# One decoder block on one core: the bias rows on GpSimd's queue head by head, and rstd spread by transposes of its repeated column

## The chip, the core and the metric

The kernel runs on one core of a Trainium2 chip. The core has five engines that run side by side, each through its own instruction stream in order: TensorE (PE, with its weight loads listed as PEld), VectorE (DVE), ScalarE (ACT), GpSimd (POOL) and SyncE (SP). They meet through semaphores. Sixteen DMA engines move data between DRAM and the core's memory; transfers are handed to them by the streams of SP and POOL. The metric is the device time of one execution in microseconds; less is better.

## What is computed

One layer of a decoder trunk on 512 tokens of width 1024, all in float32. Cut to what matters here:

```python
h = rmsnorm(x, g_pre_mix)
ca, cb, q, k, v, pu, gl = split_cols(h @ w_in)
y_conv = conv_module(ca, cb, ...)          # GLU, causal depthwise conv of 31 taps, LayerNorm, swish, 512 -> 1024
o = diff_attention(q, k, v, rel_bias, lam_p, subln_g)
    # 4 heads, two softmax maps each; logits = q k^T / 8 + rel_bias[bucket(i - j)], causal
    # attn = softmax_0 - lambda * softmax_1;  o = rmsnorm(attn @ v, subln_g) * (1 - lambda_init)
y_pool = pool_mixer(pu, ...)               # causal window means of 2, 4, 8, 16 tokens, minus the token
merged = sigmoid(gates) * (y_conv, o @ w_attn_out, y_pool), summed
x = x + rmsnorm(merged @ w_out, g_post_mix)
x = x + rmsnorm(relu(rmsnorm(x) @ w_mlp_in)**2 @ w_mlp_out, g_post_mlp)
x = x + sigmoid(x @ w_ple_gate) * (p @ w_ple_proj)
```

The bias of a head depends on the distance i - j alone, so one row of 512 numbers per head holds it. Each rmsnorm and the LayerNorm needs one number per token, rstd = (mean of squares + eps) ** -0.5.

## The kernel before

Activations lie with features on the 128 partitions and the 512 tokens along the free axis, so a 512 x 1024 activation is eight tiles of 128 x 512. Every matrix is cut into chunks of 128 x 1024 numbers (512 KB), 144 of them, which come in order through the class `Weights`: `load` (L71) issues a chunk's DMA on SP's queue into a tile called `raw`, and `split` (L87) makes two float32r tiles of it, `wh` by a copy on ACT (L90) and `wl`, the rest, by a subtraction on DVE (L94). There are three `raw` tiles (`N_RAW`) and three pairs `wh`/`wl` (`N_SPLIT`) in turn, so the load of chunk n waits until chunk n - 3 has been split, and the split of chunk n until TensorE is through with chunk n - 3. A product is three matmuls (`mm3`, L153 to L156): high by high, low by high, high by low.

The order of the projections is a string, `ORDER` (L16): q and k of the first head, the first two convolution chunks (side by side), V, pooling, and so on. The V projection (`project_v`, L660) uses four chunks, V0 to V3, each for all four blocks of tokens, 24 matmuls a chunk. Between the matmuls a planner (`tick`, L246) drops steps of other work into the program: attention first, the convolution's taps (L570) second. After the hand-ordered start (up to `start.close()`, L382) a list scheduler with its own estimate of times sets the order of each engine's stream; nothing is reordered on the chip.

**The bias** (L371 to L380, L427 to L433). The rows of the four heads are made by one matmul with a one-hot matrix (L374) and copied by ACT into `rel_r`, 4 x 640 numbers (L375). `rel_r` takes one of the three `raw` tiles, so a weight chunk waits until it has been read. A DMA on SP's queue writes it to DRAM as `rel_d` (L377); a second one, behind it, repeats each row 128 times into `rep_d` (L380), 4 x 128 x 640 numbers or 1.31 MB, in one instruction whose outermost dimension is the four heads. `load_bias(h)` (L427) then reads head h's 128 x 512 bias tile with a row step of 639 numbers, which shifts each row by one against the row before; the tile has two buffers. The attention's steps add it in L454 on DVE.

**rstd** (`rstd_from` L198, `rstd_steps` L206). Four matmuls with a column of ones sum the squares (L211); DVE scales and adds eps (L201); POOL raises to -1/2 (L203); then, one per 128 tokens, a float32 matmul of rstd's column, repeated 128 times as the stationary operand, against the identity puts rstd into every partition (L216). This runs eleven times: at the start, once per head, once in the LayerNorm, twice on halves of the tokens after W_out and twice after the MLP, and once before the MLP. Seven of them are of four blocks of 128 tokens, four are of two.

Of the kernel before, what the change touches and what calls it, by code (L numbers as in the profile page):

```python
# [9 lines left out]
F32 = mybir.dt.float32  # L10
# [24 lines left out]
P = 128  # L35
S = 512
# [3 lines left out]
NH = 4  # L40
# [71 lines left out]
def block_kernel(ctx: ExitStack, tc: tile.TileContext, xT, pT, wts, pool_w, par, rel_bias, onehot, out):  # L112
    nc = tc.nc
# [4 lines left out]
    ap = ctx.enter_context(tc.tile_pool(name="ap", bufs=N_ACT))  # L118
# [3 lines left out]
    dr = ctx.enter_context(tc.tile_pool(name="dr", bufs=1, space=bass.MemoryType.DRAM))  # L122
# [11 lines left out]
    def act_tile(name, dt=F32, tag=None, pool=None, n=S):  # L134
        uid[0] += 1
        tag = tag or OWN.get(name, "a")
        return (pool or ap).tile([P, n], dt, tag=tag, name=f"{name}_{uid[0]}", bufs=BUFS.get(tag))

    def bank(tag="mm"):
        uid[0] += 1  # L140
        return ps.tile([P, S], F32, tag=tag, name=f"{tag}_{uid[0]}")
# [17 lines left out]
    start = ExitStack()  # L159
# [23 lines left out]
    ident = cp.tile([P, P], F32, name="ident")  # L183
# [14 lines left out]
    def rstd_from(ssq, inv_n, n, name):  # L198

        c = small(n, name + "c")  # L200
        nc.vector.tensor_scalar(out=c, in0=ssq, scalar1=inv_n, scalar2=EPS, op0=ALU.mult, op1=ALU.add)  # L201
        r = small(n, name + "r")
        nc.gpsimd.tensor_tensor(out=r, in0=c, in1=neghalf[:, 0:n], op=ALU.pow)  # L203
        return r

    def rstd_steps(sq, lo, n, inv_n, got, tag="at"):  # L206


        b = bank(tag)
        for j in range(n):  # L210
            nc.tensor.matmul(out=b[:, j:j + 1], lhsT=sq[:, lo + j * P:lo + (j + 1) * P], rhs=ones_col,  # L211
                             start=True, stop=True)
        r = rstd_from(b[:, 0:n], inv_n, n, "pe")
        yield
        for j in range(n):
            nc.tensor.matmul(out=b[:, j * P:(j + 1) * P], lhsT=r[:, j:j + 1].to_broadcast([P, P]),  # L216
                             rhs=ident, start=True, stop=True)
        got(b[:, 0:n * P])


# [61 lines left out]
    for kt in range(2):  # L282
        h, l = act_tile("ph", F32R), act_tile("pl", F32R)
# [41 lines left out]
    chunk[0] = 2  # L325
    x_rB = []
    steps = rstd_steps(ssum, 0, 4, 1.0 / D, x_rB.append)
    next(steps)
    project_p(6)
# [5 lines left out]
    for kt in range(KT + 1):  # L335
        if kt < KT:
            nc.vector.tensor_tensor(out=x_t[kt], in0=x_t[kt], in1=x_rB[0], op=ALU.mult)  # L337
        if kt > 0:
            h, l = act_tile("xnh", F32R, "xn", xnp), act_tile("xnl", F32R, "xn", xnp)
# [31 lines left out]
    rel_r = rawp.tile([NH, 640], F32, tag="raw", name="rel_r")  # L371
    nc.vector.memset(rel_r, NEG)
    b = bank("at")
    nc.tensor.matmul(out=b[0:NH, :], lhsT=rb_sb, rhs=oh_sb, start=True, stop=True)  # L374
    nc.scalar.copy(out=rel_r[:, 0:S], in_=b[0:NH, :])  # L375
    rel_d = dr.tile([NH, 640], F32, name="rel_d")
    nc.sync.dma_start(out=rel_d, in_=rel_r)  # L377

    rep_d = dr.tile([NH, P, 640], F32, name="rep_d")
    nc.sync.dma_start(out=rep_d, in_=bass.AP(tensor=rel_d.tensor, offset=rel_d.offset, ap=[[640, NH], [0, P], [1, 640]]))  # L380

    start.close()  # L382

# [43 lines left out]
    def load_bias(h):  # L427
        t = act_tile("bias")
        src = rep_d[h]
        nc.sync.dma_start(out=t, in_=bass.AP(tensor=src.tensor, offset=src.offset + P - 1, ap=[[639, P], [1, S]]))  # L430
        return t

    biases = [load_bias(0)]  # L433

    qk = []

    def attention():
# [68 lines left out]
        def normalize(h):  # L506
            sq, o = state["o"]

            def scaled(rB):
                nc.vector.scalar_tensor_tensor(out=o, in0=o, scalar=sub_g, in1=rB, op0=ALU.mult, op1=ALU.mult)  # L510
                hl = act_tile("oh", F32R), act_tile("ol", F32R)
                mul_split(*hl, o)
                o_hl[h] = hl
            state["fin", h] = rstd_steps(sq, 0, 4, 1.0 / P, scaled)
            next(state["fin", h])
# [5 lines left out]
        for i in range(n + 3):  # L521
            h, qb = divmod(i, 4)
            if i < n:
                while len(qk) <= h:
                    yield None
                if qb == 0 and h + 1 < NH:
                    biases.append(load_bias(h + 1))
                logits(i)
                yield 2.5 * (qb + 1) / 4 + 0.2
            if 0 < i <= n:  # L530
                combine(i - 1)
                yield 0.66 * ((i - 1) % 4 + 1) / 4 + 0.2
            if 2 < i <= n + 2 and (i - 3) % 2 == 1:
                values(i - 3)
                yield 0.3
                if (i - 3) % 4 == 3:
                    normalize((i - 3) // 4)
                    yield 0.3
            if 1 < i <= n + 1:
                transpose(i - 2)  # L540
                yield 0.66 * ((i - 2) % 4 + 1) / 4 + 0.1
            if i % 4 == NORM_LAG % 4 and i >= NORM_LAG:
                finish((i - NORM_LAG) // 4)
                yield 1.4
# [32 lines left out]
    def conv_norm():  # L577
# [16 lines left out]
        yield 2.5  # L594
        c_rB = []
        steps = rstd_steps(csq, 0, 4, 1.0 / S, c_rB.append)
        next(steps)
        for z in range(WAIT_LN):
# [160 lines left out]
    for kt in range(KT):  # L759
        t = act_tile("x")  # L760
# [7 lines left out]
    def bank2():  # L768
        turn2[0] += 1
        return bank(("mm", "at")[turn2[0] % 2])  # L770
# [96 lines left out]
    def one_tile(src):  # L867
        wh, wl = next_chunk()
        b = bank2()
        for kt in range(KT):  # L870
            mm3(b, wh[:, kt * P:(kt + 1) * P], wl[:, kt * P:(kt + 1) * P], *src[kt], kt == 0, kt == KT - 1)
        return b

    f = [act_tile("f", tag=t) for t in spare]
# [26 lines left out]
    for quarter in range(4):  # L901
# [10 lines left out]
        if quarter < 3:  # L912
            for m in range(KT):
                b = one_tile(s_hl)
# [9 lines left out]
    for m in range(KT):  # L924
        t = act_tile("proj2")
# [13 lines left out]
    for m in range(4, KT - 1):  # L939
        b = one_tile(x2)  # L940
        finish(m, b, slice(0, S))
    wh, wl = next_chunk()
    for sl in HALVES:
        b = bank2()
# [115 lines left out]
```

## Time and profile before

| what | value |
|---|---|
| time, median of 3 runs | 850.94 us (849.89 to 852.63) |
| the profiled execution | 850.82 us, span on the core 849.0 us |
| PE busy | 837.4 us, 99% of the span |
| DVE busy | 505.4 us, 60% |
| ACT busy | 349.2 us, 41% |
| POOL busy | 24.2 us, 3% |
| mean granted TensorE clock | 0.996 of full speed |
| DMA | 89.11 MB, mean 105 GB/s |

The span runs from the first to the last instruction on the core; the 1.8 us by which the execution's time is longer lie around it. Times below are microseconds from the span's start. A matmul in a dense stream is listed with a duration longer than its share, because matmuls are pipelined: what counts is the distance from one start to the next, 0.23 us for 512 columns at the full clock.

### The profile page before, as it was taken

The page shows a single profiled execution, that of the slowest core. Times are in us where ns is not written, and L with a number is a line of the kernel's source. Part 1 is how long each engine was busy: PE and PEld are TensorE (multiplying, and loading weights), DVE is VectorE, ACT ScalarE, POOL GpSimd, SP SyncE. Part 2 cuts the span into 40 slices and gives each one's busy share as a digit, 9 for nine tenths or more (in the row PEclk, how much of TensorE's full clock was granted, in tenths as well). Part 3 has the DMA queues.
Part 4 walks back from the last instruction along what each step waited for, and adds up shares of the span by engine and source line. Part 5 has one row for each costly group of instructions (what it writes and reads, how often), then busy time and mean ns, then how long its engine had stood idle before and what let it go on. Part 6 is the DMA issues. An engine that isn't in the chain of part 4 may idle for free.

```text
span 849.0 us, 10743 instructions
## 1 busy us (share of the span) xinstructions
PE 837.4 (99%) x4216; PEld 710.0 (84%) x4216; DVE 505.4 (60%) x835; ACT 349.2 (41%) x564; POOL 24.2 (3%) x57
## 2 busy tenths in 40 slices
PE   9979999999999999999999999999999999999998
PEld 7758888888888888888999888888888888889997
DVE  5839769976669995658367642343344433435772
ACT  6625426464552323653455542332134312325341
POOL 2100000010000000000000000000000000000000
PEclk9989999999999999999999999999999999999999
DMA  8353322232122223256202523222222222222311
GB/s 288 130 203 114 112 100 75 74 113 75 52 79 94 76 99 100 84 190 208 89 27 80 184 68 116 100 100 100 99 96 90 89 98 100 100 74 76 125 56 69
DMA packets 27951, 89.11 MB, mean 105 GB/s; under 512 B 3160, under 2 KB 3544, under 8 KB 27900
## 3 DMA queue, kind: packets, MB, share of 16 engines
q1 hardware_dynamic: 27260, 86.32, 30.3%
q0 software_dynamic: 640, 2.10, 0.6%
q8 instruction: 33, 0.54, 0.3%
q14 instruction: 18, 0.15, 0.1%
HBM read 84.20 MB, written 5.52 MB: 106 GB/s over the span
## 4 chain that ended last, share of the span: by engine, by line
PE 96%; DMA 2%; DVE 1%; ACT 1%; SPq 0%; issue 0%; ACTq 0%
PE mm L154 21%; PE mm L155 21%; PE mm L156 21%; PE at L154 9%; PE at L155 9%; PE at L156 9%; DMA raw<-in_wts_dram 2%; PE at L216 1%; PE at L211 1%; PE at L450 1%; PE at L448 1%; PE at L481 1%; DMA p<-in_pT_dram 0%; DMA rel_d<-rel_r 0%; DVE x L337 0%; DVE xnl L150 0%
## 5 line engine op out<-in xcount | busy, mean ns | idle before, releaser
L90 ACT CAST wh<-raw 128x1024 fp32r<-128x1024 f32 (+1 forms) x144 | 148.8, 1040 | 337.8 <-PE mm L155 153.7
L94 DVE TENSOR_TENSOR wl<-raw,wh 128x1024 fp32r<-128x1024 f32 (+1 forms) x144 | 173.6, 1210 | 112.9 <-ACT wh L90 112.5
L156 PE MATMUL mm<-xnh,wl 128*128 128x512 f32 x352 | 138.0, 392 | 0.1
L155 PE MATMUL mm<-xnl,wh 128*128 128x512 f32 x352 | 137.5, 391 | 0.0
L154 PE MATMUL mm<-xnh,wh 128*128 128x512 f32 x352 | 136.9, 392 | 0.0
L570 DVE SCALAR_TENSOR_TENSOR acc<-u,par_sb,acc 128x512 f32<-128x512 f32 x116 | 82.4, 752 | 0.1
L154 PEld LDWEIGHTS mm<-xnh,wh 128*128 128x128 f32 x352 | 66.1, 188 | 14.3 <-ACT xnh L149 0.9
L156 PEld LDWEIGHTS mm<-xnh,wl 128*128 128x128 f32 x352 | 66.1, 188 | 14.2 <-DVE wl L94 0.5
L155 PEld LDWEIGHTS mm<-xnl,wh 128*128 128x128 f32 x352 | 66.1, 188 | 13.6 <-DVE xnl L150 0.4
L154 PE MATMUL mm<-sh,wh 128*128 128x512 f32 (+1 forms) x152 | 54.5, 359 | 0.0
L155 PE MATMUL mm<-sl,wh 128*128 128x512 f32 (+1 forms) x152 | 54.5, 358 | 0.0
L156 PE MATMUL mm<-sh,wl 128*128 128x512 f32 (+1 forms) x152 | 54.2, 357 | 0.0
L154 PE MATMUL at<-sh,wh 128*128 128x512 f32 (+1 forms) x144 | 53.0, 369 | 0.0
L156 PE MATMUL at<-sh,wl 128*128 128x512 f32 (+1 forms) x144 | 52.9, 367 | 0.0
L154 PE MATMUL at<-xgh,wh 128*128 128x512 f32 (+1 forms) x144 | 52.9, 367 | 0.0
L155 PE MATMUL at<-xgl,wh 128*128 128x512 f32 (+1 forms) x144 | 52.7, 366 | 0.0
L156 PE MATMUL mm<-xgh,wl 128*128 128x512 f32 (+1 forms) x144 | 52.7, 366 | 0.0
L155 PE MATMUL at<-sl,wh 128*128 128x512 f32 (+1 forms) x144 | 52.7, 368 | 0.0
L154 PE MATMUL mm<-xgh,wh 128*128 128x512 f32 (+1 forms) x144 | 52.7, 366 | 0.0
L156 PE MATMUL at<-xgh,wl 128*128 128x512 f32 (+1 forms) x144 | 52.7, 366 | 0.0
L155 PE MATMUL mm<-xgl,wh 128*128 128x512 f32 (+1 forms) x144 | 52.6, 365 | 0.0
L154 PEld LDWEIGHTS mm<-sh,wh 128*128 128x128 f32 x152 | 28.6, 188 | 4.6
(240 smaller groups left out, 1531.0 us busy)
## 6 DMA issues: line engine op xcount, KB each, us to landing
raw<-in_wts_dram SPq DMA_DIRECT2D x140, 512.0 KB, 3.2
x<-in_xT_dram SPq DMA_DIRECT2D x16, 256.0 KB, 6.1
proj_d<-proj POOLq DMA_DIRECT2D x8, 256.0 KB, 4.0
proj<-proj_d SPq DMA_DIRECT2D x8, 256.0 KB, 4.5
out_dram<-pg SPq DMA_DIRECT2D x7, 256.0 KB, 2.0
rep_d<-rel_d SPq DMA_DIRECT2D x1, 1280.0 KB
raw<-in_wts_dram SPq DMA_DIRECT2D x4, 256.0 KB, 5.3
bias<-rep_d SPq DMA_DIRECT2D x4, 256.0 KB, 4.5
```

The source lines that it names most:

```text
L90: i = self.nc.scalar.copy(out=wh[:, sl], in_=src)
L94: i = self.nc.vector.tensor_tensor(out=wl[:, sl], in0=src, in1=wh[:, sl].bitcast(F32), op=ALU.subtract)
L154: nc.tensor.matmul(out=o, lhsT=sh, rhs=mh, start=first, stop=False)
L155: nc.tensor.matmul(out=o, lhsT=sh, rhs=ml, start=False, stop=False)
L156: nc.tensor.matmul(out=o, lhsT=sl, rhs=mh, start=False, stop=last)
L211: nc.tensor.matmul(out=b[:, j:j + 1], lhsT=sq[:, lo + j * P:lo + (j + 1) * P], rhs=ones_col, start=True, stop=True)
L216: nc.tensor.matmul(out=b[:, j * P:(j + 1) * P], lhsT=r[:, j:j + 1].to_broadcast([P, P]), rhs=ident, start=True, stop=True)
L448: nc.tensor.matmul(out=lg[m][:, 0:nn], lhsT=q[m][:, cols], rhs=k[m][:, 0:nn], start=True, stop=False)
L450: nc.tensor.matmul(out=lg[m][:, 0:nn], lhsT=ql[m][:, cols], rhs=k[m][:, 0:nn], start=False, stop=True)
L481: nc.tensor.transpose(out=tp[:, j * P:(j + 1) * P], in_=e[:, j * P:(j + 1) * P], identity=ident)
L570: nc.vector.scalar_tensor_tensor(out=t, in0=u[:, k:k + S], scalar=pcol(w0 + k), in1=t, op0=ALU.mult, op1=ALU.add)
```

## The change

Two things are changed. First, the stores of the bias rows (`rel_d`), the repeats and the loads of the bias tiles are issued by GpSimd instead of SP, and the one repeat of all heads is four, each 128 x 640 numbers (328 KB) into a DRAM tile of its own; the repeat of head h + 1 is issued in the code after the load of head h. Second, the spreading matmul of `rstd_steps` becomes `nc.tensor.transpose`, the same instruction with its transpose flag on: the repeated column is the data, the identity the other operand.

```diff
@@ rstd_steps
         for j in range(n):
-            nc.tensor.matmul(out=b[:, j * P:(j + 1) * P], lhsT=r[:, j:j + 1].to_broadcast([P, P]),
-                             rhs=ident, start=True, stop=True)
+            nc.tensor.transpose(out=b[:, j * P:(j + 1) * P], in_=r[:, j:j + 1].to_broadcast([P, P]), identity=ident)
         got(b[:, 0:n * P])
@@ block_kernel
     rel_d = dr.tile([NH, 640], F32, name="rel_d")
-    nc.sync.dma_start(out=rel_d, in_=rel_r)
-
-    rep_d = dr.tile([NH, P, 640], F32, name="rep_d")
-    nc.sync.dma_start(out=rep_d, in_=bass.AP(tensor=rel_d.tensor, offset=rel_d.offset, ap=[[640, NH], [0, P], [1, 640]]))
+    nc.gpsimd.dma_start(out=rel_d, in_=rel_r)
+
+
+    rep_d = [dr.tile([P, 640], F32, name=f"rep_d{h}") for h in range(NH)]
+
+    def repeat_rows(h):
+        nc.gpsimd.dma_start(out=rep_d[h], in_=bass.AP(tensor=rel_d.tensor, offset=rel_d.offset + 640 * h,
+                                                      ap=[[0, P], [1, 640]]))
+
+    repeat_rows(0)
@@ load_bias
         src = rep_d[h]
-        nc.sync.dma_start(out=t, in_=bass.AP(tensor=src.tensor, offset=src.offset + P - 1, ap=[[639, P], [1, S]]))
+        nc.gpsimd.dma_start(out=t, in_=bass.AP(tensor=src.tensor, offset=src.offset + P - 1, ap=[[639, P], [1, S]]))
+        if h + 1 < NH:
+            repeat_rows(h + 1)
         return t
```

The scheduler then places things anew. On SP's queue, around the loads of the weight chunks of the V projection, there stood (raw_433 is V0, raw_439, raw_500 and raw_506 are V1 to V3):

```order
L76 DMA raw_384<-in_wts_dram 128x1024
L76 DMA raw_433<-in_wts_dram 128x1024
L377 DMA rel_d<-rel_r 4x640
L380 DMA rep_d<-rel_d 512x1x640
L76 DMA raw_439<-in_wts_dram 128x1024
L76 DMA raw_500<-in_wts_dram 128x1024
L76 DMA raw_506<-in_wts_dram 128x1024
L430 DMA bias_357<-rep_d 128x512
L430 DMA bias_680<-rep_d 128x512
```

In the changed kernel the same place of SP's queue reads (V0 to V3 are now raw_437, raw_443, raw_504 and raw_510):

```order
L76 DMA raw_388<-in_wts_dram 128x1024
L76 DMA raw_437<-in_wts_dram 128x1024
L76 DMA raw_443<-in_wts_dram 128x1024
L76 DMA raw_504<-in_wts_dram 128x1024
L76 DMA raw_510<-in_wts_dram 128x1024
```

Four transfers have left the queue; raw_443 takes the tile that `rel_r` held, so its load waits for the store of `rel_d` to land. On POOL's stream of the changed kernel, where before only memsets stood behind the last store of `proj_d` (the projected p), there now stands:

```order
L348 DMA proj_d<-proj_323 128x512
L417 MEMSET ql_1195 64x512
L417 MEMSET ql_1196 64x512
L376 DMA rel_d<-rel_r 4x640
L382 DMA rep_d_354<-rel_d 128x640
L382 DMA rep_d_355<-rel_d 128x640
L382 DMA rep_d_356<-rel_d 128x640
L382 DMA rep_d_357<-rel_d 128x640
L435 DMA bias_360<-rep_d_354 128x512
L435 DMA bias_684<-rep_d_355 128x512
L629 MEMSET pu_788 128x16
```

The scheduler has put all four repeats in a row; the first waits for `rel_d` to land, the first bias load for the first repeat. On TensorE, in the V projection, the first chunk's matmuls for all four blocks of tokens stood together; these are the last of V0 and the first of V1 before:

```order
L155 MATMUL mm_525<-wl_436,xnh_274 128x512
L156 MATMUL mm_525<-wh_435,xnl_275 128x512
L154 MATMUL mm_526<-wh_435,xnh_269 128x512
L155 MATMUL mm_526<-wl_436,xnh_269 128x512
L156 MATMUL mm_526<-wh_435,xnl_270 128x512
L154 MATMUL mm_526<-wh_435,xnh_274 128x512
```

At the same place, twelve matmuls after the start of V0 (wh_439), the changed kernel already wants V1 (wh_445), and twelve later one half of V2 (wh_506), before it comes back to V0:

```order
L155 MATMUL mm_529<-wl_440,xnh_274 128x512
L156 MATMUL mm_529<-wh_439,xnl_275 128x512
L154 MATMUL mm_528<-wh_445,xnh_283 128x512
L154 MATMUL mm_529<-wh_445,xnh_283 128x512
L155 MATMUL mm_528<-wl_446,xnh_283 128x512
L156 MATMUL mm_528<-wh_445,xnl_284 128x512
```

V1 is wanted twelve matmuls earlier than before; the number of matmuls is the same. On DVE, from the split of V1 on, there stood before:

```order
L94 TENSOR_TENSOR wl_442<-raw_439,wh_441 128x1024
L570 SCALAR_TENSOR_TENSOR acc_540<-u_495,par_sb,acc_540 128x512
L570 SCALAR_TENSOR_TENSOR acc_79_542<-u_495,par_sb,acc_79_542 128x512
L570 SCALAR_TENSOR_TENSOR acc_540<-u_495,par_sb,acc_540 128x512
L94 TENSOR_TENSOR wl_503<-raw_500,wh_502 128x1024
L454 ISA lg_690,mx_688<-at_682,bias_357 128x128
```

and in the changed kernel:

```order
L94 TENSOR_TENSOR wl_446<-raw_443,wh_445 128x1024
L94 TENSOR_TENSOR wl_507<-raw_504,wh_506 128x1024
L565 SCALAR_TENSOR_TENSOR u_499<-sg_501,mm_449 128x512
L577 SCALAR_TENSOR_TENSOR acc_544<-u_499,par_sb,acc_544 128x512
L461 ISA lg_695,mx_693<-at_687,bias_360 128x128
```

The first use of the bias stands right behind V2's split and one tap of the convolution; V3's split, wl_513, stands 21 rows behind it (before, wl_509 stood 10 rows behind it).

## Rows read from the trace of the kernel before

**Rows 1.** The page: busy us by engine; ACT's copies (busy, mean ns | idle before).

```profile
PE 837.4 (99%) x4216; PEld 710.0 (84%) x4216; DVE 505.4 (60%) x835; ACT 349.2 (41%) x564; POOL 24.2 (3%) x57
...
L90 ACT CAST wh<-raw 128x1024 fp32r<-128x1024 f32 (+1 forms) x144 | 148.8, 1040 | 337.8 <-PE mm L155 153.7
```

**Rows 2.** The page: the chain that ended last, share by engine.

```profile
PE 96%; DMA 2%; DVE 1%; ACT 1%; SPq 0%; issue 0%; ACTq 0%
```

**Rows 3.** Stages: length, PE, PEld, DVE, ACT, POOL busy (count); clock, DMA share, GB/s.

```profile
51.00:57.00 6.00, 0.15 (x1) 0.15 (x1) 0.17 (x1) 1.25 (x2) 0.00 (x0) 0.82 0.43 136
57.00:62.00 5.00, 5.00 (x13) 3.92 (x14) 5.00 (x10) 3.01 (x4) 0.00 (x0) 0.54 0.55 186
62.00:103.00 41.00, 41.00 (x184) 34.03 (x183) 37.48 (x74) 19.47 (x38) 0.00 (x0) 1.00 0.37 120
103.00:200.00 97.00, 97.00 (x466) 81.27 (x465) 76.65 (x147) 48.80 (x89) 5.27 (x12) 1.00 0.26 89
```

**Rows 4.** TensorE in time: start, us, line, tiles, count [idle before, releaser].

```profile
48.06 0.39 PE L154 MATMUL mm<-wh,xnh 128*128 128x512 f32 x1
...
50.55 0.39 PE L156 MATMUL mm<-wh,xnl 128*128 128x512 f32 x1
56.85 2.08 PE L154 MATMUL mm<-wh,xnh 128*128 128x512 f32 x4 [5.91 <-ACT wh L90]
...
61.91 0.39 PE L154 MATMUL mm<-wh,xnh 128*128 128x512 f32 x1
```

**Rows 5.** The chain that ended last, in time: start, us, what.

```profile
37.09 0.59 ACT rel_r L375
37.70 1.47 DMA rel_d<-rel_r
39.18 0.72 SPq L380
40.00 15.68 DMA raw<-in_wts_dram
```

**Rows 6.** SP's queue: what it waited for: us in total, times, longest.

```profile
SPq L430 <- DMA rep_d<-rel_d: 8.3, 1, 8.3
...
SPq L430 <- DVE mx L454: 3.9, 2, 2.9
```

**Rows 7.** Stages of 1 us, columns as in rows 3.

```profile
36.00:37.00 1.00, 1.00 (x6) 0.84 (x5) 0.94 (x5) 0.94 (x2) 0.00 (x0) 1.00 1.02 410
44.00:45.00 1.00, 1.00 (x6) 0.84 (x5) 0.00 (x0) 0.00 (x0) 0.00 (x0) 1.00 0.26 102
```

**Rows 8.** Spreading matmuls and attention's transposes in the chain: start, us, count.

```profile
162.87 0.44 PE at L481 x4
...
191.96 0.89 PE at L216 x8
...
430.72 0.45 PE at L216 x4
```

**Rows 9.** Stores of proj_d on POOL: ns of one issue min/median/max, first and last start.

```profile
L349 POOL DMA_DIRECT2D proj_d<-proj x8: 542/542/731, 18.3 to 33.4; - x8
```

**Rows 10.** DMAs of proj_d, eight POOL stores and eight SP loads: issue to landing.

```profile
DMA to landing us min/median/max: 2.5/4.5/5.2
```

**Rows 11.** Weight chunks, 10 to 110 us: the same column.

```profile
DMA to landing us min/median/max: 3.1/3.9/15.7
```

**Rows 12.** The bias tiles' loads: the same column.

```profile
DMA to landing us min/median/max: 4.4/4.5/4.6
```

**Rows 13.** DVE in time, from V0's split to V4's.

```profile
38.65 2.36 DVE L94 TENSOR_TENSOR wl<-raw,wh 128x1024 fp32r<-128x1024 f32 x2 [0.20 <-ACT wh L90]
...
56.83 1.23 DVE L94 TENSOR_TENSOR wl<-raw,wh 128x1024 fp32r<-128x1024 f32 x1 [9.97 <-ACT wh L90]
...
61.09 0.29 DVE L454 CUSTOM_DVE_ANT_0 lg<-at,bias 128x128 f32<-128x128 f32 x1
...
68.25 1.23 DVE L94 TENSOR_TENSOR wl<-raw,wh 128x1024 fp32r<-128x1024 f32 x1
```

## The prediction

> **What bounds the kernel now.** I read the page's busy times first, then the chain of work that ended last, then the stretches in which TensorE was not at its pace. TensorE is busy for 99% of the span and no other engine for more than 60% [rows 1], and 96% of the chain is TensorE's [rows 2]. So time comes off only where TensorE waits, runs at a lower clock, or does fewer or shorter instructions; a queue that is relieved elsewhere pays nothing.
>
> There is one place where it waits and slows. In a table by stage TensorE does one matmul in the 6 us from 51 to 57, the clock falls, and it stands at 0.54 of full speed from 57 to 62 and at 1.00 after that [rows 3]. In order of time the last matmul of the V projection's first chunk ends at 50.94 (50.55 and 0.39), and the next starts at 56.85, after 5.91 us, released by ACT's copy of the second chunk, V1 [rows 4]. The chain in order of time says why [rows 5]: ACT finishes `rel_r` at 37.68, its store lands at 39.18, SP issues the repeat, and the load of V1, issued right behind at 40.00, takes 15.68 us to land, where the median load takes 3.9 [rows 11]. SP itself waited 8.3 us for the repeat before it could load the first bias tile [rows 6]. The DMA share in those microseconds shows the cause: 0.26 and 102 GB/s, at 44, against 1.02 and 410 GB/s at 36 [rows 7]. A quarter of sixteen engines is four: the repeat with its four heads outermost runs on four of them, 1.31 MB at 102 GB/s being 12.8 us, and V1's share on those four stands behind it in the same queue.
>
> **The change, part by part.** *The stall.* The repeat leaves SP's queue, so V1's load has nothing ahead of it. It still waits for `rel_d`, since it takes `rel_r`'s tile. POOL issues that store at 37.7 when ACT is done [rows 5]; a store issue takes POOL 0.54 us, at most 0.73 [rows 9]. How long 10 KB take from POOL's queue no row shows. The lower bound is the 1.47 us that the same bytes took from SP's queue [rows 5], the upper one the 5.2 us of the slowest of the DMAs of `proj_d`, 256 KB each [rows 10]; I take their 2.5 us minimum, because the DMA engines are nearly idle then. So `rel_d` lands at 40.2 and V1's load is issued there. Alone it takes 3.9 us [rows 11]. Now it shares the engines with the repeats; 512 KB at 410 GB/s are 1.3 us, so an equal share adds 1.3 us: V1 lands at 45.4 and its copy, 1.04 us [rows 1], ends at 46.5. The new order wants it twelve matmuls after V0's start, where the trace has 48.06 [rows 4]. V1 is in time by 1.6 us, its low part (1.23 us on DVE [rows 13]) by about 0.8. V2 follows 1.3 to 2.6 us behind V1 and is wanted twelve matmuls later, at 50.8. So I forecast no stall: 5.91 us come off.
>
> *The slow clock after it.* From 56.85 to 61.91 TensorE starts twelve matmuls in 5.06 us [rows 4]; at the 0.23 us of a dense stream (184 in 41.00 us make 0.22 [rows 3], short ones among them) they would take 2.76. Without the idle stretch ahead of it the clock has no reason to fall: 2.3 us come off. Together 8.2 us.
>
> *The bias behind it.* In DVE's new order V3's split stands behind the first uses of the bias, so a late bias now holds up TensorE where it did not before. V3's low part is wanted 64 matmuls after the 48.06, at 62.6. Before, DVE took from the first L454 at 61.09 to the end of the next split behind the softmax, 69.48, or 8.4 us [rows 13], so the bias must be there by 54.2. The repeats: four issues by POOL from 40.2, to 42.4 (0.73 each: 43.1), 1.31 MB together with the three loads of V1 to V3, 1.57 MB, at 410 GB/s 7.0 us, done by 47.4; then the bias, 4.5 us from issue to landing [rows 12], by 51.9. That is 2.3 us to spare, and costs nothing. This takes all sixteen engines for a repeat of 128 rows; POOL's stores of `proj_d`, 128 rows too, ran among others at 1.02 share [rows 7].
>
> *POOL's stream.* Behind the later bias loads (heads 2 and 3, which wait until DVE is through with an earlier head) stand memsets and POOL's power step of the next rstd. Before, SP stood at the same two waits for 3.9 us in all, 2.9 at most [rows 6]; POOL is busy for 3% [rows 1], and what stands behind is made well ahead of its use. Zero, and at most 2.9 if that lead were gone.
>
> *Does DVE stand in the way?* While POOL issued the `proj_d` stores DVE was busy most of the time (0.94 at 36 [rows 7]), and the slowest issue took 0.73 us against 0.54 [rows 9]. The Trainium skill, SBUF — State Buffer, section "SBUF: two separate sides", speaks against the change here: it warns that a DMA issued from GpSimd has its descriptors written by GpSimd's cores, which DVE locks out while it runs in a two-port mode, and gives about 620 ns for such a DMA alone and about 3100 ns under a DVE copy. An estimate from that page's two figures: six issues at 2.5 us more each bring the bias 15 us later, to 67, and the time to about 854. The trace does not bear it out, by the 0.73 us above; and DVE ends a stretch of work at 41.0, after which it sat idle 9.97 us in one piece before 56.83 [rows 13].
>
> *The spreads.* A set of four spreading matmuls is eight passes and 0.89 us on TensorE; four transposes of 128 x 128 in the attention, float32 too and against the same identity, are four passes and 0.44 us; a set of two spreads is 0.45 [rows 8]. Seven sets of four save 0.45 each and four of two 0.225: 4.05 us, all on TensorE's path. The bounds are nothing, if a repeated column is fed as slowly as before, and 4.05; I take the upper, since the transposes are the same size and type.
>
> **The sum.** 850.82 of the profiled execution less 5.91, 2.3 and 4.05 is 838.6. The execution is within 0.12 us of the median, so I take 838.6 for the new median.
>
> **The rivals.** *V1 is still late.* If `rel_d` lands only after 5.2 us, at 42.9, and V1's load takes twice its 3.9, it lands at 50.7, its copy ends at 51.8, and TensorE idles 3.7 us from 48.06; with the slow clock's 2.3 that is 6.0 back: 844.6. For it: POOL's stores did take 4.5 us in the median. Against: these were 25 times as large, on busy engines. Chance 0.13.
>
> *The spreads stay at eight passes.* The change would not do what it says there: 842.6. Chance 0.05.
>
> *The bias comes last.* `rel_d` at 42.9, the issues at 0.73, a repeat as slow as the slowest load (15.7 us) and 4.5 for the bias: 66.0. TensorE then waits for V3's split from 62.6 to 74.4, 11.8 us, with 2.3 of slow clock behind: 852.7, no change. Against: that landing was the four-engine queue itself. Chance 0.06.
>
> *Few engines for a repeat* (slower). If the descriptors that POOL makes for a source with row step zero go to few engines at 102/4 = 25.6 GB/s each, four engines give 12.8 us from 41, the bias at 58.5 and a stall of 4.3, with the clock 6.6: 845.2. Two engines take 25.6 us, the bias lands at 71, TensorE waits 17, and with the clock's 2.3 the time is 858. It passes the time before once the stall is over 9.9 us, so below three engines. For it: the old repeat used four of sixteen. Against: its outermost dimension was four, the new one's is 128. Chance 0.04 for the slower side.
>
> *The transposes let the clock fall.* If after each of eleven sets the clock fell as after the stall, 2.3 us each, 25 us come back: 864. The attention's 40 transposes lie in stages with the clock at 1.00 [rows 3], which speaks against it. The Trainium skill, TensorE: Matmul & The Clock Gate, Part 4, holds that a transpose does not count as TensorE being busy; by that rule this rival would be likelier, but the sets last 0.44 us between dense matmuls, and the trace does not agree with a fall. Chance 0.01.
>
> **How the numbers follow.** The forecast has 0.71. The range reaches up to a late V1 and to four engines, 845.5, and down to 837.0, about what the runs scatter; that holds the forecast, the late V1 and the eight passes, 0.89 in all and less what I don't see. Within 0.3% (848.4 to 853.5, about what a measurement of this kernel can tell from no change) lies the late bias, 0.06. Slower are few engines and the clock, 0.05. Faster 0.89.
>
> **What would show it.** In the profile after, TensorE's order of time without a gap between 45 and 68 and the clock at 1.00 there; V1's load landing in about 5 us; the repeats with a DMA share near 1 from 41 to 48; the first bias use on DVE near 52; L216 with half its count and 0.44 us a set. It would be wrong if TensorE waits for ACT's copy of V1 or DVE's split of V3, which the idle time of their matmuls names, or if L216 keeps its count.

## The result, and the profile after

| | before | changed |
|---|---|---|
| time, median | 851.03 us (849.89 to 852.63, 4 runs) | 840.22 us (839.25 to 841.20, 4 runs) |
| span of the profiled execution | 849.0 us | 837.8 us |
| mean granted TensorE clock | 0.996 | 0.999 |

The ratio is 0.9877, 95% interval 0.9858 to 0.9896: faster by 10.8 us where 12.2 had been forecast; the time lies in the range, 1.6 us above the forecast.

The page of the changed kernel, its span, the busy times, and the chain's shares, beside [rows 1, 2]:

```profile
span 837.8 us, 10679 instructions
...
PE 830.7 (99%) x4180; PEld 703.5 (84%) x4180; DVE 504.8 (60%) x835; ACT 348.7 (42%) x564; POOL 29.1 (3%) x66
...
PE 93%; DVE 3%; issue 1%; DMA 1%; POOL 1%; ACT 0%; SPq 0%; POOLq 0%
```

TensorE lists 36 matmuls fewer, and 3% of the chain is now DVE's, where it was 1%. The stages, columns as in [rows 3]:

```profile
46.00:51.00 5.00, 5.00 (x24) 4.14 (x23) 1.92 (x2) 1.85 (x3) 1.39 (x6) 1.00 1.02 416
51.00:57.00 6.00, 6.00 (x28) 4.99 (x27) 5.18 (x16) 2.92 (x11) 0.00 (x0) 1.00 0.40 145
57.00:62.00 5.00, 5.00 (x23) 4.13 (x22) 5.00 (x12) 3.12 (x6) 0.00 (x0) 1.00 0.09 18
62.00:95.00 33.00, 31.73 (x141) 26.04 (x140) 30.28 (x55) 15.47 (x27) 0.68 (x2) 1.00 0.37 125
```

From 51 to 57 TensorE does 28 matmuls instead of one, and from 57 to 62 it does 23 instead of 13, at the full clock: the stall and the slow stretch are gone. A new gap stands between 62 and 95, 1.27 us in one piece. The chain shows where it comes from (start, us, what):

```profile
37.64 1.83 DMA rel_d<-rel_r
...
46.54 6.00 DMA bias<-rep_d
...
52.57 0.29 DVE lg L461
...
66.85 1.99 DVE acc L577 x3
68.83 0.61 DVE vl L150
69.49 0.51 PE mm L154
```

The bias lands at 52.54, DVE works through the first attention steps, convolution taps and weight splits in its row, and reaches the low part of V's first output (`vl`) at 68.83. Until that is made, the bank (the piece of TensorE's output memory) that holds V's sums is not free, and the next projection wants it. TensorE's row at that place, as in [rows 4]:

```profile
67.82 0.40 PE L457 MATMUL at<-k,ql 128*128 128x512 f32 x1
69.49 0.51 PE L154 MATMUL mm<-xnh,wh 128*128 128x512 f32 x1 [1.27 <-DVE vl L150]
```

The spreads, with the least, median and greatest duration in ns, answer to [rows 8]: 36 where 72 were listed, weight loads of 135 ns where the median was 190; the kernel before first, the changed one below:

```profile
L216 PEld LDWEIGHTS at<-ident,per x72: 185/190/192, 18.4 to 804.4; 128*128 128x128 f32 x72
L216 PE MATMUL at<-ident,per x72: 270/275/376, 18.5 to 804.5; 128*128 128x128 f32 x72
...
L216 PEld LDWEIGHTS at<-ident,per x36: 133/135/137, 18.6 to 793.3; 128*128 128x128 f32 x36
L216 PE MATMUL at<-ident,per x36: 270/272/323, 18.6 to 793.4; 128*128 128x128 f32 x36
```

The chain lists seven sets of four (start, us), here the first two:

```profile
18.76 0.54 PE at L216 x4
...
184.77 0.44 PE at L216 x4
```

ACT's copies of V1 and V2 (start, us, idle time before) show when their loads landed, at 43.28 and 47.57:

```profile
43.28 1.05 ACT L90 CAST wh<-raw 128x1024 fp32r<-128x1024 f32 x1 [4.03 <-DMA raw<-in_wts_dram]
47.57 1.05 ACT L90 CAST wh<-raw 128x1024 fp32r<-128x1024 f32 x1 [3.24 <-DMA raw<-in_wts_dram]
```

### The profile page after: what moved, and what is told of

The parts are those of the page before. It is cut to its first block, busy times and chain, and to the rows that moved or that the text cites. A ratio compares the mean times of both kernels' runs of the same rounds, so it can differ in the third digit from the quotient of the medians.

```text
span 837.8 us, 10679 instructions
## 1 busy us (share of the span) xinstructions
PE 830.7 (99%) x4180; PEld 703.5 (84%) x4180; DVE 504.8 (60%) x835; ACT 348.7 (42%) x564; POOL 29.1 (3%) x66
## 4 chain that ended last, share of the span: by engine, by line
PE 93%; DVE 3%; issue 1%; DMA 1%; POOL 1%; ACT 0%; SPq 0%; POOLq 0%
PE mm L154 21%; PE mm L155 20%; PE mm L156 20%; PE at L154 10%; PE at L155 10%; PE at L156 9%; DVE acc L577 1%; PE at L211 1%; DMA bias<-rep_d 1%; PE at L488 1%; PE at L457 0%; PE at L455 0%; PE at L216 0%; DVE x L336 0%; DVE wl L94 0%
```

## The experiments

The theory at this point: the gain has two parts that add up, the repeat no longer on four of the DMA engines ahead of V1's load, and the spreads at half their passes; and the new wait behind the V projection takes 1.27 us of it back. The rivals: that one part gave it all; that leaving SyncE's queue, not the form of the repeat, did it; and, for the new wait, that DVE has too much work there whatever the bias does. The first four kernels below ran on one chip beside the kernel before, the last three on another chip, so between the two groups the ratios to the kernel before are what is compared.

### Each part alone

Without the transposes (the bias rows as in the changed kernel):

```diff
-            nc.tensor.transpose(out=b[:, j * P:(j + 1) * P], in_=r[:, j:j + 1].to_broadcast([P, P]), identity=ident)
+            nc.tensor.matmul(out=b[:, j * P:(j + 1) * P], lhsT=r[:, j:j + 1].to_broadcast([P, P]),
+                             rhs=ident, start=True, stop=True)
```

> The bias rows on GpSimd's queue head by head, the spread of rstd still by fp32 products. Theory (the two parts add up, each on TensorE's path): the stall in the V projection (5.9 us) and the slow clock after it (2.3 us) stay away, the new 1.27 us wait behind the V projection stays, and the spreads cost their eight passes: 840.2 + 4.05 = 844.3 us. Rival (the spreads lie beside other work and the queue gave it all): 840 to 841 us.

Measured: 843.75 us, ratio 0.9933 (0.9921 to 0.9945), 6.7 us less than the 850.48 of the kernel before on that chip. TensorE's gaps from 24 us on are one:

```profile
70.99 0.50 PE L154 MATMUL mm<-xnh,wh 128*128 128x512 f32 x1 [2.33 <-DVE vl L150]
```

The stall is gone here too, and the wait behind V is 2.33 us, where 1.27 had been expected. The profiled execution took 846.58 us, 2.8 more than the median, so this is not the wait of a usual one. DVE's row at the first use of the bias says what differs; in the changed kernel (the second line) the idle time is 0.27:

```profile
54.06 0.29 DVE L462 CUSTOM_DVE_ANT_0 lg<-at,bias 128x128 f32<-128x128 f32 x1 [1.97 <-DMA bias<-rep_d]
...
52.57 0.29 DVE L461 CUSTOM_DVE_ANT_0 lg<-at,bias 128x128 f32<-128x128 f32 x1 [0.27 <-DMA bias<-rep_d]
```

The transposes alone (the bias rows as before the change): the same diff the other way round, in the kernel before.

> Only the spread by transposes, all bias DMAs on SyncE's queue as before. Theory: the stall and the slow clock are as before, 11 sets save 4.05 us: 851.0 - 4.05 = 847.0 us, L216 36 instead of 72 matmuls. Rival (the spreads lie beside other work): 851 us. Rival (transposes let TensorE's clock fall): above 851 us, with a granted clock under 1.00 in stretches other than the one before.

Measured: 845.95 us, ratio 0.9956 (0.9944 to 0.9968), 4.5 us less. Its stages (stretch, length, TensorE busy and count, clock, DMA share, GB/s):

```profile
51.00:57.00 6.00, 0.84 (x4) 0.85 0.38 139
57.00:62.00 5.00, 4.18 (x10) 0.50 0.66 236
...
95.00:830.00 735.00, 735.00 (x3746) 1.00 0.29 97
```

Its one long gap, in TensorE's row (start, us, what, in brackets the idle time before it and what ended it):

```profile
57.82 2.07 PE L154 MATMUL mm<-wh,xnh 128*128 128x512 f32 x4 [5.98 <-ACT wh L90]
```

Stall and slow clock stand as before, and from 95 to 830, where all sets of transposes but the first lie, the clock is 1.00: it did not fall behind them. By the medians the parts give 6.7 and 4.5, together 11.3, against 10.8 of the whole change; by the ratios 5.7 and 3.7, together 9.4, against 10.5. They add up within the intervals, and that either part gave it all is ruled out.

### Queue or form

The changed kernel with every bias DMA back on SyncE's queue, the repeat still one per head:

```diff
-    nc.gpsimd.dma_start(out=rel_d, in_=rel_r)
+    nc.sync.dma_start(out=rel_d, in_=rel_r)
...
-        nc.gpsimd.dma_start(out=rep_d[h], in_=...)
+        nc.sync.dma_start(out=rep_d[h], in_=...)
...
-        nc.gpsimd.dma_start(out=t, in_=...)
+        nc.sync.dma_start(out=t, in_=...)
```

> As the changed kernel, but all bias DMAs go through SyncE's queue; the repeat stays one per head, 128 rows outermost. Theory (the stall came from the repeat running on four of sixteen DMA engines, not from SyncE's queue as such): each repeat moves 328 KB at some 410 GB/s in 0.8 us, V1's load lands by 46 us, no stall and no slow clock; the bias lands before 50 us, so that the 1.27 us wait behind the V projection goes too: 838.5 to 840.5 us. Rival (whatever stands ahead of V1's load in its queue holds it up): a stall of 3 to 6 us stays, 844 to 848 us.

Measured: 839.26 us, ratio 0.9876 (0.9862 to 0.9891), the changed kernel's own. The stages, columns as for the kernel with the transposes alone, show no stall:

```profile
51.00:57.00 6.00, 6.00 (x28) 1.00 0.38 124
57.00:62.00 5.00, 5.00 (x24) 1.00 0.33 105
```

The wait behind V, in TensorE's row, is shorter, though not gone as had been expected:

```profile
68.12 0.50 PE L154 MATMUL mm<-xnh,wh 128*128 128x512 f32 x1 [0.49 <-DVE vl L150]
```

With the repeat in this form the queue did not matter to the time. The other way round, GpSimd's queue with the repeat in its old form:

```diff
-    rep_d = [dr.tile([P, 640], F32, name=f"rep_d{h}") for h in range(NH)]
...
+    rep_d = dr.tile([NH, P, 640], F32, name="rep_d")
+    nc.gpsimd.dma_start(out=rep_d, in_=bass.AP(tensor=rel_d.tensor, offset=rel_d.offset, ap=[[640, NH], [0, P], [1, 640]]))
```

> As the changed kernel, but the repeat is again one DMA with the four heads outermost, on GpSimd's queue. Theory (four engines, 102 GB/s): V1's load is in time, but the repeat takes about 13 us from 40 us on, the first bias tile lands near 60 us, 7.5 us later than in the changed kernel, and TensorE waits behind it in or behind the V projection, with the slow clock after a long wait: 846 to 850 us. Rival (being off SyncE's queue is enough, the form of the repeat does not matter): 840 us.

Measured: 848.49 us, ratio 0.9981 (0.9973 to 0.9990). This kernel has the transposes, which alone took 845.95: so the bias rows off SyncE's queue, in the old form, gain nothing and cost 2.5 us more, though the repeat stands ahead of no weight load. The repeat in its chain (start, us, what):

```profile
39.83 21.62 DMA rep_d<-rel_d
```

One microsecond under the repeat, as a stage (stretch, length, clock, DMA share, GB/s):

```profile
56.00:57.00 1.00, 1.00 0.26 110
```

The same microsecond by queue, with the share of the 16 engines at the end; q0 carries GpSimd's transfers, q1 SyncE's:

```profile
q0 software_dynamic: 11, 0.06, 13.5%
q1 hardware_dynamic: 11, 0.05, 10.9%
```

DVE's first use of the bias (in brackets the idle time before it and what ended it):

```profile
64.65 0.29 DVE L454 CUSTOM_DVE_ANT_0 lg<-at,bias 128x128 f32<-128x128 f32 x1 [11.91 <-DMA bias<-rep_d]
```

TensorE's gaps behind it, in its row:

```profile
68.43 0.79 PE L155 MATMUL mm<-wl,xnh 128*128 128x512 f32 x1 [6.65 <-DVE wl L94]
78.92 0.80 PE L154 MATMUL mm<-xnh,wh 128*128 128x512 f32 x1 [1.99 <-DVE vl L150]
```

The share is a quarter again, and nearly half of it goes to weight loads that are left in the same quarter. The repeat takes 21.62 us where 13 had been expected, the bias is first used at 64.65, and TensorE waits for V3's split, 6.65 us, since DVE sat idle for the bias ahead of it. So the four engines cost more off SyncE's queue than on it; the victim changed from V1's load to the bias itself.

What is left is whether the number of DMAs plays a part. The kernel before, with the transposes, and its one repeat on SyncE's queue with the two outer dimensions swapped:

```diff
-    nc.sync.dma_start(out=rep_d, in_=bass.AP(tensor=rel_d.tensor, offset=rel_d.offset, ap=[[640, NH], [0, P], [1, 640]]))
+    nc.sync.dma_start(out=bass.AP(tensor=rep_d.tensor, offset=rep_d.offset, ap=[[640, P], [640 * P, NH], [1, 640]]),
+                      in_=bass.AP(tensor=rel_d.tensor, offset=rel_d.offset, ap=[[0, P], [640, NH], [1, 640]]))
```

> All bias DMAs on SyncE's queue and one repeat for all heads, as before the change, but with the 128 rows as its outermost dimension and the four heads inside (the destination the same); the spread by transposes. TensorE's order is the one of before the change. Theory (the outermost dimension alone decides how many engines a repeat takes): 1.31 MB on sixteen engines in some 3.2 us, V1's load lands near 47 us, before TensorE wants it at 50.9 in that order, no stall and no slow clock: 838.5 to 840.5 us. Rival (one long DMA ahead of V1 in its queue, or a source row read 128 times by all engines at once, is what costs): a stall of 3 us or more stays, 843 to 847 us.

Measured: 839.18 us, ratio 0.9873 (0.9859 to 0.9888); the changed kernel on the same chip, below, 838.96. One line against the kernel with the transposes alone, and TensorE waits 0.21 us instead of 5.98. The repeat in the list of DMA issues (KB, median us to landing), and ACT's copy of V1 behind it, whose load landed at 48.84, before the 50.9 at which the expectation has it wanted:

```profile
rep_d<-rel_d SPq DMA_DIRECT2D x1, 1280.0 KB, 7.8
...
48.84 1.05 ACT L90 CAST wh<-raw 128x1024 fp32r<-128x1024 f32 x1 [2.33 <-DMA raw<-in_wts_dram]
```

The repeat took 7.8 us, not the 3.2 that had been expected.

One microsecond under it, as a stage (stretch, length, clock, DMA share, GB/s):

```profile
41.00:42.00 1.00, 1.00 0.81 251
```

TensorE's one gap behind V:

```profile
69.12 0.50 PE L154 MATMUL mm<-xnh,wh 128*128 128x512 f32 x1 [0.21 <-DVE vl L150]
```

So it is shown: the outermost dimension of the repeat, four or 128, makes the first part of the gain. GpSimd's queue and the split by heads were only the way in which the change came by the other form. That it is four engines is read from the share of 0.26, not counted engine by engine.

### The wait behind V

The changed kernel with the one-hot matmul, its copy, the store and the repeats moved into the hand-ordered start, and `rel_r` in a tile of its own:

```diff
     project_p(7)
+    rel_b = bank("at")
+    nc.tensor.matmul(out=rel_b[0:NH, :], lhsT=rb_sb, rhs=oh_sb, start=True, stop=True)
+    nc.scalar.copy(out=rel_r[:, 0:S], in_=rel_b[0:NH, :])
...
     for m, t in stores:
+        if m == 4:
+            nc.gpsimd.dma_start(out=rel_d, in_=rel_r)
+            for h in range(NH):
+                repeat_rows(h)
         nc.gpsimd.dma_start(out=proj_d[m], in_=t)
```

> As the changed kernel, but the one-hot matmul, its copy, the store of rel_d and the four repeats stand in the hand-ordered start, some 15 us earlier, and rel_r has a tile of its own, so that V1's load waits for none of it. The scheduler then puts the first attention steps on DVE behind the split of V's outputs. Theory (the 1.27 us wait behind the V projection came from DVE being late with V's low parts, held up by the bias and the softmax ahead of them): that wait is gone, 838.5 to 839.5 us. Rival (DVE has too many convolution taps there whatever the bias does): a wait of 0.5 to 1.5 us stays, 839.5 to 841 us. A third possibility: the repeats collide with the weight loads of the start and cost 1 to 3 us there, 840 to 843 us.

Measured: 840.08 us, ratio 0.9887 (0.9872 to 0.9902), above the 838.5 to 839.5 that had been expected. DVE reaches `vl` earlier and TensorE has no gap behind V; but there are two new ones at the start. TensorE's row there:

```profile
22.73 0.51 PE L154 MATMUL mm<-xnh,wh 128*128 128x512 f32 x1 [1.29 <-ACT xnh L149]
23.52 0.50 PE L155 MATMUL mm<-xnl,wh 128*128 128x512 f32 x1 [0.28 <-DVE xnl L150]
```

DVE's row at `vl`, which ended the wait at 69.44 in the changed kernel:

```profile
67.58 0.68 DVE L150 SCALAR_TENSOR_TENSOR vl<-mm,vh 128x512 fp32r<-128x512 f32 x1
```

ACT's row says where the first new gap comes from. The copy of `rel_r` stands ahead of the first `xnh`, and ACT sat idle 2.60 us in front of it, until TensorE had done the one-hot product; in the changed kernel on the same chip the first `xnh` starts at 19.42:

```profile
21.48 0.57 ACT L337 COPY rel_r<-at 4x512 f32<-4x512 f32 x1 [2.60 <-PE at L336]
21.96 1.33 ACT L149 ACTIVATE xnh<-x,par_sb 128x512 fp32r<-128x512 f32 x2
```

Behind the two new gaps the clock fell (stretch, length, TensorE busy and count, clock, DMA share, GB/s):

```profile
24.00:26.00 2.00, 2.00 (x7) 0.54 0.24 95
26.00:28.00 2.00, 2.00 (x7) 0.61 0.67 123
28.00:30.00 2.00, 2.00 (x10) 1.00 0.82 201
```

From 24 to 28 TensorE does 14 matmuls where about 20 fit by the row below. The 1.27 us are DVE's and go when the attention's first steps stand behind `vl`. In the profiled execution (840.85 us) what was won was given back at the start, in the two waits and the slow clock behind them. The copy's place in ACT's row did that, and not the repeats: GpSimd issued the first of them at 25.60, behind both gaps. Two of the four executions took 839.3 us at a mean clock of 1.00, so the slow clock is not part of each; the intervals of this kernel and of the changed one overlap, and all that is shown is that nothing was gained.

The changed kernel again, beside the last two:

> The changed kernel as it is, beside the other two on the same chip: 840.2 us, the wait behind the V projection between 0.5 and 2.5 us. Both theories expect the same; it is the base that the other two are held against.

Measured: 838.96 us, ratio 0.9874 (0.9857 to 0.9890), with a wait of 1.12 us. On this chip the kernel before takes 849.74 us; the difference is 10.8 us, as in the result. No kernel was faster than the changed one by more than the intervals.

## Why the prediction was right, point by point

*What bounds the kernel, and the cause of the stall.* Right, and shown by the swapped dimensions: a repeat on four engines, with V1's share behind it.

*The stall (5.91) and the slow clock (2.3).* Both gone, as forecast. The steps under it were conservative: `rel_d` took 1.83 us from POOL's queue, not 2.5, and V1 landed at 43.28, not 45.4, against 47.74 when the changed kernel wants it (48.06 in the forecast).

*The bias behind it.* Forecast to land by 51.9, it landed at 52.54. That this is so close is partly luck: the forecast had the load wait for all four repeats (7.0 us) and then take 4.5 us; it waited for the first repeat alone, which took 6.8, and then took 6.00, and `rel_d` was there 0.7 us earlier. V3's split was done at 60.5 (59.32 and 1.22 on DVE), before the 62.6. That the margin was real is shown by the kernel with four engines on GpSimd's queue, where the same wait is 6.65 us. But "costs nothing" is the step that failed: I followed DVE's row only to V3's split. Behind it stand another eight taps and two splits, and then `vl`, on which the next projection's bank hangs; DVE came to it 1.27 us late. Before the change TensorE's stall of 5.91 us left DVE more time; that no wait stood there for that reason was not shown, and the kernel with the swapped dimensions, with neither that stall nor the new order, waits only 0.21. The gap starts at 68.22, just behind the 45 to 68 in which the forecast said to look for one.

How much of the 1.27 us is the bias's? DVE was idle for it for 0.27 us, and for 1.97 in the kernel without transposes, where the wait is 2.33. From the first use of the bias on, DVE has no idle time until `vl`, so what the bias loses comes on top. The repeats on sixteen engines were also slower than the 410 GB/s I used (see below). But in the kernel on SyncE's queue the bias was first used 3.8 us earlier, DVE had no idle time for it, and 0.49 us of wait stayed: the row itself is too long for that place, and putting `vl` ahead of the attention's steps removed the wait.

*The spreads.* Six sets at 0.44 us, the first at 0.54, and four of half the count: 4.05 us as in the forecast; alone 4.5 us by the medians and 3.7 by the ratio (2.7 to 4.8). Right, with the upper bound as taken.

*The sum.* 5.91, 2.3 and 4.05 less the 1.27 make 11.0; the spans differ by 11.2, the medians by 10.8. The overlooked wait is about what is missing from 12.2; it was 1.12 us in a second profile of the same kernel.

*The rivals.* V1 was not late. The spreads have 36 entries, not 72. The issues of the bias DMAs on POOL took 0.53 to 0.60 us; so what the Trainium skill, SBUF — State Buffer, section "SBUF: two separate sides", warns of (DVE holding up descriptors that GpSimd writes) did not show here. It was not put to a hard test: DVE was busy for 0.94 of the 2.09 us in which the repeats were issued, and the forecast's row at 36 lies behind the last of the stores that it is held against (in the stores' own stretches of the kernel before, DVE was busy for 1.60 of 2.40 and 1.39 of 2.20 us). The clock did not fall after transposes, 1.00 from 95 to 830 in the kernel with the transposes alone. The rule of the Trainium skill, TensorE: Matmul & The Clock Gate, Part 4, that they do not count as TensorE being busy, is neither borne out nor refuted by that: a true wait of 0.49 us, as long as a set, left the clock at 1.00 as well. The price for a repeat on four engines off SyncE's queue, 845.2, was too low: 848.49, since the repeat took 21.62 us, not 12.8, with weight loads in the same quarter of the engines, and a second wait of 1.99 us came behind the first.

## What to carry to other kernels

Look at the DMA share while a long transfer runs: a flat quarter means four engines of sixteen, and whatever is next in that queue waits for those four; from another queue weight loads shared the same quarter (13.5% and 10.9% above). Putting the large dimension outermost cured it on either queue, and another queue alone did not. When a stall of the bounding engine is removed, follow each other engine's row past the next use to the one after it: here DVE was in time at the first and 1.27 us late at the second. A product that only moves numbers can be a transpose, at half the passes in float32.

## What the runs showed of the hardware

A repeat from DRAM to DRAM with all engines reading the same 10 KB ran at 251 GB/s at a share of 0.81 (one DMA, SyncE's queue), some 19 GB/s for each busy engine, where four engines made 102 GB/s at 0.26, 25 GB/s each [rows 7]. While the four-engine repeat ran ahead in SyncE's queue, the share stayed at 0.26 or less until 46, although V1's load was issued right behind it, at 40.00 [rows 5]. In the kernel before, by stage (stretch, length, TensorE busy and count, clock, DMA share, GB/s):

```profile
45.00:46.00 1.00, 1.00 (x6) 1.00 0.26 102
46.00:47.00 1.00, 1.00 (x6) 1.00 0.89 154
```

Why V1's part on the free engines did not start earlier is not shown. A store of 10 KB took 1.83 us from GpSimd's queue and 1.47 from SyncE's [rows 5].

TensorE's clock fell after shorter waits than the one before the change. After single waits of 0.21, 0.49, 1.12 and 1.27 us behind V it stayed at 1.00, but after 1.29 and 0.28 us close together at the start (the kernel with the bias early) it went to about half; after 1.99 us (the kernel with four engines on GpSimd's queue) and 2.33 us (the one without transposes) it went to half. In the kernel with the transposes alone it also stood at 0.50 from 8 to 10 us, behind waits of 0.52, 0.22 and 0.51 us between 4.5 and 7.0. By stage, the first line behind the 1.99 us, the others around the 2.33 us (columns as in the start of the kernel with the bias early):

```profile
80.00:82.00 2.00, 2.00 (x6) 0.50 0.05 17
...
70.00:72.00 2.00, 1.01 (x4) 0.90 0.81 304
72.00:74.00 2.00, 2.00 (x6) 0.50 0.00 1
74.00:76.00 2.00, 2.00 (x8) 0.75 0.00 0
76.00:78.00 2.00, 2.00 (x11) 1.00 0.71 246
```

From 72 to 76 there are 14 matmuls where 22 fit at the last row's rate, so the wait of 2.33 us cost by my estimate some 1.5 us more behind it. How much of the difference between these places is the length of the wait, and how much the work around it, was not tried.
